# Mixture-of-experts stage: weights in row quarters of 1024 columns, gate before up, joins over two blocks

## The chip, the core and the metric

The kernel runs on one core of a Trainium2 chip. The metric is the device time of one execution in microseconds, as the median of three runs. The engines are TensorE (PE, matmul), VectorE (DVE), ScalarE (ACT), GpSimd (POOL) and SyncE (SP, which here only issues transfers).

## What is computed

One layer of a decoder, fp32 in and out, 1024 tokens of width 1024: normalisation and projection, two groups of attention heads, an output projection, and then a mixture of 32 experts, of which each token takes 4. The change lies in the experts:

```python
def moe_ffn(h, w_router, b_router, w_gate_up, b_gate_up, w_down, b_down):
...
    logits = (h @ w_router).astype(jnp.float32) + b_router.astype(jnp.float32)
    top_val, top_idx = lax.top_k(logits, TOP_K)
    gates = jax.nn.softmax(top_val, axis=-1)
...
    def expert_block(args):
        xe, e = args
        gu = xe @ w_gate_up[e] + b_gate_up[e]
        g = jnp.minimum(gu[:, :D_FF], SWIGLU_LIMIT)
        u = jnp.clip(gu[:, D_FF:], -SWIGLU_LIMIT, SWIGLU_LIMIT)
        act = (u + 1.0) * (g * jax.nn.sigmoid(SWIGLU_ALPHA * g))
        return act @ w_down[e] + b_down[e]
...
    y = yb[dest] * gate_sorted[:, None].astype(yb.dtype)
    return jax.ops.segment_sum(y, tok_sorted, num_segments=n)
```

The layer's output is `x + gate2 * y`, with `gate2` (the second gate) a row of 1024 that comes from the layer's condition `c`.

## The kernel before

**Stages.** The first 590 us or so are the projection and the attention, then come output projection and router by blocks of 128 tokens, which end in a list of tokens for every expert, and from about 743 us on the experts run one after the other. The order of the experts is by their load (`seq`), and each place in it has a fixed number of columns (tokens) `C`, from 200 down to 96 (`CAPS`). The order alternates, mostly a large one and a small one: 15 experts have at most 128 columns, that is one block, 17 have more, that is two blocks. The last one in time has 96.

**One expert.** `stage_g` gathers the rows of its tokens (POOL). `stage_t` turns them by PE transposes, four per bank of PSUM, and makes the operand `xx` out of them: ACT copies the high part, DVE subtracts to get the low part, POOL casts `xb`. `first_products` multiplies 512 rows x 512 columns of weights at a time (`kh` = 0, 1) into four banks: four high products per column block with `xx`, which carries high and low part side by side (2C columns, at least 256), and four low products with `xb` (C columns). A half of 512 columns of gate is followed by the same half of up, then the second halves follow. `joined` (L1177 to L1183) puts a block of sums together: ACT adds the bias into `tb` (L1179), DVE adds `tb` and the high sums (L1181, L1183). Gate goes through a sigmoid, two blocks at once (L1197, L1198). Down takes the raw fp32 weights (L1220; two records in the trace for each matmul), in two passes `kh` over two column halves, and after the first pass `between()` calls `stage_t` for the next expert. ACT empties the sums of down into `yT` (L1225). `back` turns `yT` back (L1237), DVE multiplies by the token's weight and by `gate2` (L1239), and POOL scatters into `out` with addition (L1153). `back` is put off to the first `done` of the next expert.

**Weights.** A chunk is 512 rows x 512 columns, 1 MB, issued by SP (`load_chunk`, L782). Chunks of gate and up have 5 tiles (`eraw`), those of down 4 (`draw`). A chunk of gate or up is split in two steps (`split_half`): ACT writes the high half (L796), DVE the low half in bf16 (L797), into 12 slots. `done(c)` runs after each chunk's products: it gives the chunk free and calls `pump`, which issues loads as long as tiles are free and writes up to one split (two after a chunk of down).

**Order.** In the expert stage PE, ACT, DVE and SP keep the order in which the program is written; POOL's order is the planner's.

Of the kernel before, what the change touches and what calls it, by code (L numbers as in the profile page):

```python
# [9 lines left out]
F32 = mybir.dt.float32  # L10
# [10 lines left out]
P = 128  # L21
# [37 lines left out]
ND = 4  # L59
# [7 lines left out]
TB = 2  # L67
# [6 lines left out]
NC_ = 512  # L74
# [3 lines left out]
def hybrid_layer(ctx: ExitStack, tc: tile.TileContext, x, c_t, w_ada, b_ada_t, b_ada, norm1_t, w_in,  # L78
# [11 lines left out]
    modd = dram.tile([3, D], F32, name="modd")  # L90
# [30 lines left out]
    def rsqrt_mean(*a):  # L121
# [18 lines left out]
    gate2 = consts.tile([P, D], F32, name="gate2")  # L140
# [43 lines left out]
    with ExitStack() as st:  # L184
        with ExitStack() as sp:
# [164 lines left out]
            def mod_row(n, acc):  # L350
# [11 lines left out]
                def rest():  # L362
                    if v == 3:
                        nc.vector.tensor_add(gate2[:, cs], pb, bb)
                        return
# [154 lines left out]
        with ExitStack() as so:  # L520
# [139 lines left out]
            m2 = rt.tile([P, 2, KT], F32, name="m2")  # L660
            wr = rt.tile([P, KT, E], F32, name="wr")
# [101 lines left out]
            at_ = {"dma": 0, "split": 0, "use": 0, "open": 0}  # L763
            raws, held = {}, {"eraw": 0, "draw": 0}
            pools = {"eraw": (wraw, NRAW)}
# [6 lines left out]
            def kind_of(d):  # L772
                return "eraw" if d % NCH < NGU else "draw"

            def load_chunk():
                d, kind = at_["dma"], kind_of(at_["dma"])
                i, w, n, kh = CHUNKS[d]
# [3 lines left out]
                raws[d] = pools[kind][0].tile([P, 4, NC_], F32, name=kind, bufs=pools[kind][1])  # L781
                nc.sync.dma_start(raws[d], w[ds(e, 1), kh * 512:(kh + 1) * 512, n * NC_:(n + 1) * NC_]  # L782
                                  .rearrange("o (k p) n -> p (o k) n", p=P))
                held[kind] += 1
                at_["dma"] += 1

            def split_half():

                t = at_["split"]
                c, q = t // 16 * NCH + t % 16 // 2, t % 2  # L790
                raw = raws[c][:, 2 * q:2 * q + 2]
                h_ = slot(False).rearrange("p (k n) -> p k n", k=2)
                if q == 0:
                    parts[c] = [], slot(True).bitcast(BF16).rearrange("p (k n) -> p k n", k=4)
# [625 lines left out]
```

## Time and profile before

| | us |
|---|---|
| median of 3 runs (2167.42 to 2168.32) | 2167.44 |
| the profiled execution | 2167.32 |
| its span, first to last instruction | 2165.5 |
| PE busy in the span | 2094.8 |
| DVE busy | 1499.6 |
| ACT busy | 1150.2 |
| POOL busy | 429.3 |

The profile is one execution on the chip. A line of a group gives source line, engine, operation, the tile written and the tiles read, the shape, the count, the busy time and the mean length of one instruction. A line of the timeline gives start and length of a run of like instructions, their count, and in brackets how long the engine had stood idle before and what ended that. The lengths of consecutive matmuls overlap in the timeline, so their pace is read from start to start. A view of stretches gives the busy time of every engine between two moments, the clock granted to PE, the busy share of the transfer engines and their rate.

### The profile page before, as it was taken

How to read it: one execution, taken by the hardware profiler on the slowest of the kernel's cores; microseconds unless marked ns; L12 is line 12 of the kernel's file. 1: busy time of each engine (PE TensorE's matmuls, PEld its weight loads, DVE VectorE, ACT ScalarE, POOL GpSimd, SP SyncE). 2: the span in 40 equal slices, each digit the busy share in tenths (PEclk: the TensorE clock that was granted, in tenths of full speed). 3: DMA queues.
4: the chain of work that ended last, by engine and by line, in shares of the span. 5: the costliest groups of instructions: out<-in, count | busy, mean ns of one | idle time of the engine just before them, and what ended most of it. 6: DMA issues, size and time to landing. Idle time of an engine off the chain costs nothing. (4 is left out here: it accounts for less than half of the span.)

```text
span 2165.5 us, 43655 instructions
## 1 busy us (share of the span) xinstructions
PE 2094.8 (97%) x16922; PEld 1957.5 (90%) x16922; DVE 1499.6 (69%) x2946; ACT 1150.2 (53%) x2263; POOL 429.3 (20%) x444
## 2 busy tenths in 40 slices
PE   7999999999999699999999999999999999999997
PEld 6877778998777699999999999999999999999997
DVE  6587756776666876677667677776767767667763
ACT  3522224777633455566456565656556656656652
POOL 2255532111045401111011111110111101101100
PEclk9999999999999799999999999999999999999999
DMA  7267886442224598799799999989989989999882
GB/s 294 73 163 215 221 230 172 114 109 76 89 105 153 192 356 299 247 334 350 255 292 326 300 314 319 332 312 343 315 297 312 361 297 320 323 315 335 297 320 60
DMA packets 272404, 548.98 MB, mean 254 GB/s; under 512 B 30675, under 2 KB 30691, under 8 KB 272067
## 3 DMA queue, kind: packets, MB, share of 16 engines
q1 hardware_dynamic: 250323, 490.09, 65.4%
q0 software_dynamic: 21872, 56.08, 11.1%
q8 instruction: 134, 2.20, 0.4%
q14 instruction: 75, 0.61, 0.1%
HBM read 501.31 MB, written 44.77 MB: 252 GB/s over the span
## 5 line engine op out<-in xcount | busy, mean ns | idle before, releaser
L797 DVE TENSOR_TENSOR ha<-eraw,hb 128x1024 bf16<-128x1024 f32 x512 | 601.3, 1224 | 233.5 <-ACT hb L796 233.0
L1167 PE MATMUL gu<-xx,hb 128*128 128x256 f32 (+13 forms) x4096 | 641.5, 304 | 0.6 <-DVE xx L1149 0.6
L1167 PEld LDWEIGHTS gu<-xx,hb 128*128 128x128 f32 x4096 | 561.1, 190 | 1.0 <-DVE xx L1149 0.8
L796 ACT ACTIVATE hb<-eraw 128x1024 fp32r<-128x1024 f32 x512 | 506.7, 1053 | 34.1 <-DMA eraw<-in_w_gate_up_dram 34.0
L1220 PE MATMUL gu<-aa,draw 128*128 128x128 f32 (+19 forms) x4096 | 521.2, 288 | 0.0
L1220 PEld LDWEIGHTS gu<-aa,draw 128*128 128x128 f32 x4096 | 511.2, 191 | 0.6
L1171 PE MATMUL gu<-xb,ha 128*128 128x128 bf16 (+19 forms) x4096 | 316.2, 224 | 0.0
L1179 ACT ACTIVATE tb<-gu,bcol 128x128 f32<-128x128 f32 (+19 forms) x512 | 164.6, 371 | 253.8 <-PE gu L1171 225.7
L1171 PEld LDWEIGHTS <-ha 128*128 128x128 bf16 x4096 | 246.6, 98 | 28.4 <-issue 3.3
L1153 POOL DMA_INDIRECT out_dram<-y,slot x47 | 81.6, 1736 | 528.3 <-DVE y L1239 251.4
L1126 POOL DMA_INDIRECT xg<-h2d,slot x47 | 54.5, 1160 | 629.0 <-PE gu L1146 381.8
L1225 ACT ACTIVATE yT<-gu,bcol 128x128 f32<-128x128 f32 (+19 forms) x256 | 82.4, 374 | 126.6 <-PE gu L1220 126.5
L572 DVE CUSTOM_DVE_ANT_0 p<-pss,bias 128x1024 f32<-128x1024 f32 (+7 forms) x128 | 94.4, 755 | 49.5 <-ACT p L581 22.2
L606 PE MATMUL po<-vsb,pT 128*128 128x64 f32 (+1 forms) x864 | 111.1, 275 | 2.6 <-ACT pT L600 1.5
L606 PEld LDWEIGHTS po<-vsb,pT 128*128 128x128 f32 x864 | 105.6, 194 | 4.8 <-ACT pT L600 1.8
L581 ACT ACTIVATE p<-p,mn 128x1024 f32<-128x1024 f32 (+7 forms) x128 | 98.6, 773 | 12.8 <-DVE mn L572 12.1
L1197 ACT ACTIVATE sg<-gt 128x256 f32<-128x256 f32 (+19 forms) x128 | 55.8, 436 | 89.2 <-DVE gt L1183 89.2
L461 PE MATMUL pp<-wh,hb 128*128 128x512 f32 x240 | 101.7, 424 | 0.0
L1198 DVE TENSOR_TENSOR gt<-gt,sg 128x256 f32<-128x256 f32 (+19 forms) x128 | 57.4, 448 | 63.4 <-ACT sg L1197 63.4
L112 POOL TENSOR_TENSOR rrs<-vrs,nhalf 128x8 f32<-128x8 f32 (+2 forms) x48 | 66.6, 1386 | 165.3 <-DVE vrs L110 160.2
L463 PE MATMUL pp<-wl,hb 128*128 128x512 f32 x240 | 94.9, 395 | 0.0
L462 PE MATMUL pp<-wh,hb 128*128 128x512 f32 x240 | 94.8, 395 | 0.0
(265 smaller groups left out, 2623.6 us busy)
## 6 DMA issues: line engine op xcount, KB each, us to landing
eraw<-in_w_gate_up_dram SPq DMA_DIRECT2D x256, 1024.0 KB
draw<-in_w_down_dram SPq DMA_DIRECT2D x128, 1024.0 KB
wraw<-in_w_ada_dram SPq DMA_DIRECT2D x32, 512.0 KB
wraw<-in_w_in_dram SPq DMA_DIRECT2D x23, 512.0 KB
hb<-in_w_ada_dram SPq DMA_DIRECT2D x16, 512.0 KB
qd<-tt POOLq DMA_DIRECT2D x32, 256.0 KB, 4.0
kd<-tt POOLq DMA_DIRECT2D x32, 256.0 KB, 4.2
ha<-qd SPq DMA_DIRECT2D x32, 256.0 KB
```

Source lines behind the costliest of these rows:

```text
L461: nc.tensor.matmul(pp, hh[b][:, k], wh[:, kk], start=(k == 0), stop=False)
L462: nc.tensor.matmul(pp, hl[b][:, k], wh[:, kk], start=False, stop=False)
L463: nc.tensor.matmul(pp, hh[b][:, k], wl[:, kk], start=False, stop=(k == KT - 1))
L572: nc.vector.tensor_tensor_reduce(p[:, :n], pss[:, :n], bias[:, (NB - 1 - ib) * P:(NB - 1 - ib) * P + n], -1.0, 3.0e38, OP.add, OP.min, mn)
L581: nc.scalar.activation(p, p, AF.Exp, bias=self.mn[c], scale=-1.0, accum_out=self.l[:, c:c + 1])
L606: nc.tensor.matmul(self.po[:, :w], self.pT[:, k], vsb[self.br][:, k, self.h * w:(self.h + 1) * w], start=(k == 0), stop=(k == self.ib))
L796: nc.scalar.activation(h_, raw, AF.Copy)
L797: nc.vector.tensor_tensor(l_, raw, h_.bitcast(F32), OP.subtract)
L1167: nc.tensor.matmul(pg[j][:, :max(256, 2 * C)], w[k][0][:, j * P:(j + 1) * P], xx[4 * kh + k], start=(kh + k == 0), stop=False)
L1171: nc.tensor.matmul(pg[j][:, C:2 * C], w[k][1][:, j * P:(j + 1) * P], xb[:, 4 * kh + k], start=False, stop=(kh == 1 and k == 3))
L1179: nc.scalar.activation(t, p[:, C:2 * C], AF.Identity, bias=bias, scale=1.0)
L1220: nc.tensor.matmul(p, w[:, k, j * P:(j + 1) * P], a[:, 4 * kh + k], start=(kh + k + j % 2 == 0), stop=(kh == 1 and k == 3 and j % 2 == 1))
```

## The change

Seen from the code, it does this:

- A chunk is now 256 rows x 1024 columns, still 1 MB. All kinds of chunks share one ring of 7 tiles. Gate and up have four chunks each per expert, down four. A split takes one half of a chunk's columns.
- Both halves of gate come first, then both halves of up. A product call (`products`) uses the splits of one column half from all four quarters of the rows.
- The low half of split t is written behind the high half of split t + 1. The number of splits that `pump` may write after each of the 12 `done()` events of an expert stands in the table `TG`.
- Tiles of PSUM are two banks. `joined` handles two blocks at once on DVE, the sigmoid four. `back` makes eight transposes and one evacuation, on ACT, with the token's weight as scale.
- `gate2` enters as scale and in the bias when ACT empties the sums of down (`g2c`, loaded from a fourth row of `modd`). The full row `gate2` is loaded only for the overflow stage at the end.
- Down goes by quarters of the rows over all 1024 columns. `between(0)` after the second quarter makes the first four transposes of each block of the next expert, `between(1)` after the fourth makes the other four and then `xx` and `xb`.
- `N3` is 0, so the code that stands under `if N3` and the terms with `N3` have no effect.

```diff
-ND = 4
+NRING = 7
+TG = (12, 12, 14, 16, 17, 18, 19, 20, 22, 24, 26, 27)
+N3 = 0
...
-    gate2 = consts.tile([P, D], F32, name="gate2")
-
-
-
-    CHUNKS0 = [(w_gate_up, 2 * u + half, kh) for half in range(2) for u in range(2) for kh in range(2)] + \
-              [(w_down, n, kh) for kh in range(2) for n in range(2)]
+
+
+
+    CHUNKS0 = [(w_gate_up, u, kq) for u in range(2) for kq in range(4)] + [(w_down, 0, kq) for kq in range(4)]
     NGU, NCH = 8, len(CHUNKS0)
+    NSP = 2 * NGU + (NCH - NGU if N3 else 0)
...
+                nc.sync.dma_start(g2c, modd[3].rearrange("(k p) -> p k", p=P))
...
+            def room():
+
+                d = at_["dma"]
+                p = pools.get(d % NRING >= NRAW)
+                return p if d < len(CHUNKS) and p and (d < NRING or d - NRING in freed) else None
...
+                raws[d] = pool.tile([P, 2, FF], F32, name=name, bufs=n)
+                nc.sync.dma_start(raws[d], w[ds(e, 1), kq * 256:(kq + 1) * 256, u * FF:(u + 1) * FF]
                                   .rearrange("o (k p) n -> p (o k) n", p=P))
...
+            def low(t):
+                c, half = chunk_of(t)
+                nc.vector.tensor_tensor(parts[t][1], raws[c][:, :, half * 512:(half + 1) * 512], parts[t][0].bitcast(F32), OP.subtract)
+                give(c, 1)
...
+                nc.scalar.activation(h_, raws[c][:, :, half * 512:(half + 1) * 512], AF.Copy)
+                if t:
+                    low(t - 1)
+                if t == E * NSP - 1:
+                    low(t)
...
+            def pump(upto):
+
                 while True:
-                    d, t = at_["dma"], at_["split"]
-                    kind = kind_of(d)
-                    if d < len(CHUNKS) and kind in pools and held[kind] < pools[kind][1]:
+                    if room():
                         load_chunk()
-                    elif t < limit and t // 16 * NCH + t % 16 // 2 < d and at_["open"] < NH:
+                    elif at_["split"] < upto and splittable():
                         split_half()
                     else:
                         return
...
+        def done(*ts):
+
+            used.update(ts)
+            for t in ts:
+                parts.pop(t)
+            i, q = divmod(event[0], len(TG))
+            event[0] += 1
+            pump(i * NSP + TG[q])
             for t in todo:
                 t[0] -= 1
             while todo and todo[0][0] <= 0:
...
+        def stage_t(st, g):
+
+            C = st["C"]
+            if g == 0:
+                st["x"], st["pt"] = operand(C, "xx", "xb"), []
+                bc = st["bc"]
+                nc.vector.tensor_mul(bc[:, 2 * KT:], bc[:, 2 * KT:], g2c)
+            xx, xb, _ = st["x"]
+            for (t0, n), xg in zip(st["blocks"], st["xg"]):
+                if g == 0:
+                    st["pt"].append(banks().rearrange("p g (k c) -> p (g k) c", k=4))
+                pt = st["pt"][t0 // P]
+                for k in range(4 * g, 4 * g + 4):
+                    nc.tensor.transpose(pt[:, k, :n], xg[:n, k * P:(k + 1) * P], ident[:n, :n])
+                if g:
+                    d_ = xx[:, :, t0:t0 + n]
                     nc.scalar.activation(d_, pt[:, :, :n], AF.Copy)
-                    nc.vector.tensor_sub(xx[:, 4 * g:4 * g + 4, C + t0:C + t0 + n], pt[:, :, :n], d_.bitcast(F32))
-                    nc.gpsimd.tensor_copy(xb[:, 4 * g:4 * g + 4, t0:t0 + n], d_.bitcast(F32))
+                    nc.vector.tensor_sub(xx[:, :, C + t0:C + t0 + n], pt[:, :, :n], d_.bitcast(F32))
+                    nc.gpsimd.tensor_copy(xb[:, :, t0:t0 + n], d_.bitcast(F32))
...
-        def joined(dst, p, C, bias, more=0.0):
-            t = ap_.tile([P, C], F32, name="tb", bufs=TB)
-            nc.scalar.activation(t, p[:, C:2 * C], AF.Identity, bias=bias, scale=1.0)
-            if more:
-                nc.vector.scalar_tensor_tensor(dst, t, more, p[:, :C], op0=OP.add, op1=OP.add)
-            else:
-                nc.vector.tensor_add(dst, p[:, :C], t)
-
...
+            def joined(dst, p, f, more):
+
+                t = ap_.tile([P, 2, C], F32, name="tb", bufs=2)
+                for j in range(2):
+                    nc.scalar.activation(t[:, j], p[:, j, C:2 * C], AF.Identity, bias=bc[:, f + j:f + j + 1], scale=1.0)
+                if more:
+                    nc.vector.scalar_tensor_tensor(dst, t, more, p[:, :, :C], op0=OP.add, op1=OP.add)
+                else:
+                    nc.vector.tensor_add(dst, p[:, :, :C], t)
...
+                ts = of(0, half)
+                pg = products(C, st["x"], ts)
+                gt = ap_.tile([P, 4, C], F32, name="gt", bufs=2)
                 for q in range(2):
+                    joined(gt[:, 2 * q:2 * q + 2], pg[q], 4 * half + 2 * q, 0.0)
+                sg = ap_.tile([P, 4, C], F32, name="su")
+                nc.scalar.activation(sg, gt, AF.Sigmoid, scale=1.702)
+                nc.vector.tensor_mul(gt, gt, sg)
+                gts.append(gt)
+                done(*ts[2:])
...
+            for kq in range(4):
+                raw = raws[d0 + kq]
+                for j in range(KT - N3):
+                    for k in range(2):
+                        nc.tensor.matmul(place(j), raw[:, k, j * P:(j + 1) * P], a[:, 2 * kq + k],
+                                         start=(kq + k + j % 2 == 0), stop=(kq == 3 and k == 1 and j % 2 == 1))
+                give(d0 + kq, 1 if N3 else 2)
...
+                    nc.gpsimd.tensor_copy(ab[:, f:f + 4], ah[:, f:f + 4, :C].bitcast(F32))
+                if kq == 3:
+                    for j in range(KT - N3):
+                        nc.scalar.activation(yT[:, j], place(j), AF.Identity,
+                                             bias=bc[:, 2 * KT + j:2 * KT + j + 1], scale=g2c[:, j:j + 1])
+                done()
+                if kq % 2:
+                    between(kq // 2)
...
+                    py = banks().rearrange("p g (k c) -> p (g k) c", k=4)
+                    for k in range(KT):
+                        nc.tensor.transpose(py[:n, k], yT[:, k, r0:r0 + n], ident)
+                    nc.scalar.activation(y[:n].rearrange("p (k c) -> p k c", k=KT), py[:n], AF.Copy, scale=sl[:n, 1:2])
...
-            expert(st, lambda: nxt and stage_t(nxt))
+            expert(i, st, lambda g: nxt and stage_t(nxt, g))
```

## Rows read from the trace of the kernel before

**Rows 1.** Page's busy table, and PE in the 40 slices of the span.
```profile
PE 2094.8 (97%) x16922; PEld 1957.5 (90%) x16922; DVE 1499.6 (69%) x2946; ACT 1150.2 (53%) x2263; POOL 429.3 (20%) x444
...
PE   7999999999999699999999999999999999999997
```

**Rows 2.** Stretches: length, busy PE, PEld, DVE, ACT, POOL (counts), PE clock, DMA share, GB/s.
```profile
743.00:2152.00 1409.00, 1409.00 (x13054) 1375.68 (x13054) 982.75 (x1623) 814.05 (x1499) 184.95 (x201) 1.00 0.90 307
```

**Rows 3.** Page's costliest groups: low halves of splits, high products, down.
```profile
L797 DVE TENSOR_TENSOR ha<-eraw,hb 128x1024 bf16<-128x1024 f32 x512 | 601.3, 1224 | 233.5 <-ACT hb L796 233.0
L1167 PE MATMUL gu<-xx,hb 128*128 128x256 f32 (+13 forms) x4096 | 641.5, 304 | 0.6 <-DVE xx L1149 0.6
...
L1220 PE MATMUL gu<-aa,draw 128*128 128x128 f32 (+19 forms) x4096 | 521.2, 288 | 0.0
```

**Rows 4.** Timeline, 180-column expert into 124-column: start, length, engine, line, operands, count [idle before].
```profile
1241.07 1.01 PE L1146 MATMUL gu<-ident,xg 124*128 124x124 f32 x8
1241.76 1.06 ACT L1148 ACTIVATE xx<-gu 128x496 fp32r<-128x496 f32 x2 [3.60 <-PE gu L1146]
...
1241.92 9.93 PE L1220 MATMUL gu<-aa,draw 128*128 128x180 f32 x64
1242.37 1.26 DVE L1149 TENSOR_TENSOR xx<-gu,xx 128x496 fp32r<-128x496 f32 x2 [1.24 <-ACT xx L1148]
...
1251.56 2.20 PE L1167 MATMUL gu<-xx,hb 128*128 128x256 f32 x16
1251.88 0.71 ACT L1225 ACTIVATE yT<-gu,bcol 128x180 f32<-128x180 f32 x2 [1.67 <-PE gu L1220]
...
1252.49 2.97 ACT L796 ACTIVATE hb<-eraw 128x1024 fp32r<-128x1024 f32 x3
```

**Rows 5.** Transfers: a first load, its use, and the rate of a stretch.
```profile
1.21 5.06 SPq L294 DMA_DIRECT2D hb<-in_w_ada_dram  x9
...
5.12 0.49 DVE L229 TENSOR_SCALAR acc<-hb,sc 128x512 f32<-128x512 f32 x1 [2.32 <-DMA hb<-in_w_ada_dram]
...
26.00:28.00 2.00, 2.00 (x11) 2.00 (x11) 2.00 (x2) 0.00 (x0) 2.00 (x1) 1.00 1.08 421
```

**Rows 6.** PE's clock at the head of the stage: stretches, then PE's timeline.
```profile
717.00:717.50 0.50, 0.00 (x0) 0.00 (x0) 0.50 (x2) 0.43 (x1) 0.30 (x1) 1.00 0.00 0
...
720.50:721.00 0.50, 0.50 (x4) 0.50 (x4) 0.43 (x3) 0.15 (x1) 0.49 (x1) 0.50 1.02 418
...
746.00:748.00 2.00, 2.00 (x12) 1.76 (x11) 2.00 (x2) 2.00 (x3) 1.16 (x1) 0.57 0.33 51
...
742.77 4.96 PE L1167 MATMUL gu<-xx,hb 128*128 128x344 f32 x16 [0.65 <-DVE xx L1149]
...
752.62 2.75 PE L1167 MATMUL gu<-xx,hb 128*128 128x344 f32 x16
```

**Rows 7.** PE's timeline of a 124-column expert: steps of up, down.
```profile
1165.29 2.15 PE L1167 MATMUL gu<-xx,hb 128*128 128x256 f32 x16
...
1168.15 1.21 PE L1167 MATMUL gu<-xx,hb 128*128 128x256 f32 x8
...
1182.74 7.36 PE L1220 MATMUL gu<-aa,draw 128*128 128x124 f32 x64
1189.93 1.67 PE L1146 MATMUL gu<-ident,xg 128*128 128x128 f32 x16
```

**Rows 8.** Timeline of gate's evacuation at 124 columns.
```profile
1260.45 0.60 ACT L1179 ACTIVATE tb<-gu,bcol 128x124 f32<-128x124 f32 x2
1260.58 0.42 DVE L1198 TENSOR_TENSOR gt<-gt,sg 128x248 f32<-128x248 f32 x1 [0.48 <-ACT sg L1197]
1260.91 0.47 DVE L1183 TENSOR_TENSOR gt<-gu,tb 128x124 f32<-128x124 f32 x2
...
1261.42 0.41 ACT L1197 ACTIVATE sg<-gt 128x248 f32<-128x248 f32 x1 [0.37 <-DVE gt L1183]
```

More of the change, by code (lines that the diff above doesn't have):

```diff
@@ L66 @@
 BORD = (7, 5, 3, 1, 0, 2, 4, 6)
-TB = 2
 CAP0 = 172
@@ L762, in hybrid_layer @@
             parts, reg = {}, {0: 0}
-            at_ = {"dma": 0, "split": 0, "use": 0, "open": 0}
-            raws, held = {}, {"eraw": 0, "draw": 0}
-            pools = {"eraw": (wraw, NRAW)}
+            at_ = {"dma": 0, "split": 0}
+            raws, freed, used = {}, set(), set()
+            pools = {0: (wraw, NRAW, "eraw")}
             def expert_of(i):
@@ L785, in load_chunk, with give, chunk_of, splittable @@
                 at_["dma"] += 1
+            def give(d, n):
+                left[d] = left.get(d, 2) - n
+                if left[d] == 0:
+                    raws.pop(d)
+                    left.pop(d)
+                    freed.add(d)
+            left = {}
+            def chunk_of(t):
+                i, r = divmod(t, NSP)
+                return (i * NCH + r // 2, r % 2) if r < 2 * NGU else (i * NCH + r - NGU, 1)
+            def splittable():
+                t = at_["split"]
+                return t < E * NSP and chunk_of(t)[0] < at_["dma"] and (t < NH or (t - NH in used and (t - NH) | 1 in used))
@@ L1185, in expert, with of @@
-        def expert(st, between):
+                    done(*ts[:2])
+            return pg
+        def expert(i, st, between):
             C, bc = st["C"], st["bc"]
             a = ap_.tile([P, KT, C], F32, name="aa")
+            s_a = operand(C, "ax", "ab") if N3 else None
+            t0, d0 = i * NSP, i * NCH + NGU
+            gts = []
+            def joined(dst, p, f, more):
[6 more added lines that the diff above has]
+                    nc.vector.tensor_add(dst, p[:, :, :C], t)
+            def of(u, half):
+                return [t0 + 8 * u + 2 * kq + half for kq in range(4)]
@@ L1200, in expert @@
-                done(c)
-                c, pg = first_products(st)
+                    joined(gt[:, 2 * q:2 * q + 2], pg[q], 4 * half + 2 * q, 0.0)
[4 more added lines that the diff above has]
+                done(*ts[2:])
+            for half in range(2):
+                ts = of(1, half)
+                pg = products(C, st["x"], ts)
+                ut_ = ap_.tile([P, 4, C], F32, name="su")
@@ new lines, in expert @@
+            if N3:
+                ts = [t0 + 2 * NGU + kq for kq in range(4)]
+                pg = products(C, s_a, ts)
+                for j in range(4):
+                    f, p = 4 + j, pg[j // 2][:, j % 2]
+                    t = ap_.tile([P, 2, C], F32, name="tb", bufs=2)[:, 0]
+                    nc.scalar.activation(t, p[:, C:2 * C], AF.Identity, bias=bc[:, 2 * KT + f:2 * KT + f + 1], scale=g2c[:, f:f + 1])
+                    nc.vector.scalar_tensor_tensor(yT[:, f], p[:, :C], g2c[:, f:f + 1], t, op0=OP.mult, op1=OP.add)
+                done(*ts[2:])
@@ L1298, in hybrid_layer @@
         lists(0)
-        pump(PB - at_["split"])
+        pump(PB)
         st = stage_g(0)
-        stage_t(st)
+        stage_t(st, 0)
+        stage_t(st, 1)
         lists(1)
-        pump(NH - at_["open"])
+        pump(TG[-1] - NSP)
         mans.close()
```

156 lines of the change are left out of this document (47 added, 109 removed).

## Prediction

> **What bounds the kernel now.** I looked first for the engine without slack. The page's busy table and its 40 slices give TensorE (PE) 97% of the span, and from the fifteenth slice on PE shows nine tenths or more in every slice [rows 1]. The view of stretches sharpens this: from 743 to 2152 us PE is busy 1409.00 us of 1409.00, at a granted clock of 1.00 [rows 2]. That stretch is the expert stage, 65% of the span, and nothing in it makes PE wait. Next comes what is in those 1409 us. By the groups of costliest instructions they are above all the high products of gate and up (L1167) and the down products (L1220), with 4096 records each [rows 3]; the low products (L1171) and the transposes come behind them. The change leaves every one of these matmuls, with its column count, in place: two records for each fp32 matmul of down, 256 matmuls of gate and up and 8 to 16 transposes in and out per expert. It follows that **there is nothing to win inside the stage**: the change can only alter the 756 us outside it or open holes in a full engine. So I read the rest of the trace for one purpose: what stands between the end of one expert and the first product of the next, and how much room it has.
>
> In the kernel before that room is large. The timeline of an expert with 180 columns followed by one with 124 shows the 8 transposes of the next expert's rows at 1241.07 in the middle of down, the two copies (ACT) and the two subtractions (DVE) that make its operand `xx` done by 1243.63, and the first product of the next expert only at 1251.56 [rows 4]. The operand is ready 8 us early.
>
> **The change part by part.** *Edits with no effect on PE.* DVE loses 2 of 4 joins per half and the `y` products with the gate; ACT gains one 1024-element evacuation per block. Neither engine is the bound (983 and 814 us of 1409 [rows 2]), and their work lies beside the products, so the saving is worth nothing; what covers it is the full PE. The rows of 4 KB instead of 2 KB for weights are worth nothing either: DMA moves 307 GB/s on average in the stage [rows 2] while PE waits for none of it, and rows of 2 KB reached 421 GB/s in the opening stage [rows 5]. The one extra write of `modd` on POOL, the small load `g2c` on SP and the late load of `gate2` lie in stages whose PE does not wait for those queues; with the longer first evacuation I put 2 us on start and end together (bounds 0 and 6; the start's own row is the 0.65 us of idle ahead of 742.77 [rows 6]).
>
> *The operand of the next expert.* This is the part that decides. `stage_t` is now called twice: four transposes per block after the second quarter of down, the other four **after the last one**, and only then the copy to `xx`, the subtraction and POOL's cast. PE runs in written order, and the next thing written on PE is the first gate product, which reads `xx`. Nothing else lies between: `back` comes only at the first `done` of the next expert. So at each of 31 expert boundaries PE stands still for a chain on ACT and DVE. Count it from the last down matmul, at the boundary of [rows 4] (T = 1251.56). ACT takes up the last pair of `yT` 0.32 us after T and needs 0.71: T+1.03. The `done()` that stands ahead of the second `stage_t` lets `pump` write one more weight split (limit 26 to 27), and ACT is served in order: + 0.99 (2.97 for 3): T+2.02. Copy to `xx` of 8 x 124: at most the two old copies, 1.06: T+3.08. Subtraction, likewise 1.26: T+4.34. PE meanwhile does four transposes, half of the 0.85 us that 8 took (1241.07 to 1241.92): 0.43. **Hole: 3.9 us.** For a following expert of two blocks another short copy and subtraction and another four transposes come in, which nearly cancel.
>
> After an expert of at most 128 columns the chain is longer, since a quarter of down is then short: 64 records in 7.2 us (1182.74 to 1189.93 [rows 7]), so 3.6 us for a quarter. The ring has 7 weight tiles, and the chunk that is split after quarter 3 can be requested only when quarter 2's predecessor has set its tile free, one quarter ahead. From issue to use a half-megabyte load took 3.9 us on an empty queue (1.21 to 5.12 [rows 5]); another half megabyte at 421 GB/s adds 1.2: 5.1 us, an estimate from these rows. So ACT gets the chunk 1.5 us after the quarter's end, splits two halves (2.0), does eight `yT` at about 0.3 (2.5) and stands at 6.0 where it would have been at 4.6. Hole: 3.9 + 1.4 = 5.3 us. With 14 boundaries after small experts and 17 after large: 14 x 5.3 + 17 x 3.9 = **140 us**. Bounds: 31 x 2.9 = 90 (the split out of the way) and 31 x 5.3 = 164.
>
> *The joins, and splits one step late.* The sigmoid now waits for all four blocks, and the low half of a split is written one split later. The second half of the first up product needs the low half of split 14, which `pump` writes after the sigmoid of the second gate half. At 124 columns: ACT's last pair 0.60, join 0.47, sigmoid over 496 elements about 0.6 and product about 0.7 (the halves take 0.41 and 0.42), then two low halves of 1.2 each [rows 3, 8]: 4.9 us after the gate's end. PE gets there after 16 + 16 matmuls (1165.29 to 1168.15 [rows 7]) and 8 more (half of the 2.15 for 16): 3.9. Hole 1.0 us. At 180 columns the sums are 5.5 and 5.3. With 15 experts at 1.0 and 17 between 0 and 0.6: **20 us**, bounds 0 and 40.
>
> *The clock.* After a hole PE may not run at its old rate. In the head of the stage the granted clock was 0.50 (1.2 GHz, the lower of its two levels) from 720.5 on; before that PE had no work at all from 717.0 to 717.5. It came back between 746 and 748, after PE had been at work from 742.77 without a pause [rows 6]. Under the lower clock a run of 16 products of 344 columns is 4.96 us long, at the full clock 2.75 [rows 6]: 2.2 us lost by one recovery. If each hole costs one, 31 x 2.2 = **68 us**; if none does, 0. No row shows dense work, one hole of 4 us and dense work again, so both ends stay; I take the full price, because the fall at 720.5 came without a hole of this length just ahead of it.
> The Trainium skill, "TensorE: Matmul & The Clock Gate", section "HAM oscillation — how this bites in real kernels", says the same of loops in which each pass ends with a wait: the clock falls in every pass and the slow restart is paid each time. By that rule the sum has the 68 us; without it, it hasn't. That a single hole in dense work does it, no run here shows yet.
>
> *Sum.* 140 + 20 + 68 + 2 = 230 us. The profiled execution took 2167.32 us (span 2165.5), 0.1 us from the median 2167.44, so I add to the median: **2397 us**.
>
> **The rivals.** *The clock holds* (everything else as above): 2167 + 162 = 2329 us. For it: in [rows 6] PE found the clock still at 1.00 while it stood, and lost it only 3 us later. Against it: a hole here is eight times the empty half microsecond of that row.
>
> *The loads starve the stage.* The ring falls from 9 tiles to 7, and `pump` frees none between the fifth step and the first quarter of down, so six chunks go out together at an expert's end. Six chunks and the next are 7.3 MB: 17.4 us at 421 GB/s [rows 5], 23.9 at the 307 GB/s that the stage now moves [rows 2]. The split that wants the seventh comes after five steps, some 16 us for 124 columns plus the hole. At 421 GB/s it waits hardly at all; at 307, 3 to 5 us, and PE behind it. 31 x 3 = 93 us or more on top: 2490 us. For it: the DMA share is already 0.90 [rows 2]. Against it: PE's holes themselves leave more time.
>
> *The boundary is covered after all* (not slower). Place: the copy to `xx` behind the last quarter. If the program that is built puts these copies before quarter 3's end, the 4.3 us chain would fit into the 3.6 to 4.9 us of a quarter, and with it the clock would hold; then 2167 to 2190 us, no difference from the point where the operand is done when PE ends down. This is also the case in which the change doesn't do what it says. Against it: ACT, DVE and PE are under the written order in this stage, and the trace of before obeys it everywhere I looked.
>
> *Part of the chain overlaps* (the split early, two thirds of a hole, clock held): 2167 + 90 = 2257 us.
>
> **How the numbers follow.** Chances: forecast 0.55 (own range 2350 to 2440), clock holds 0.25 (2285 to 2350), starved 0.08 (2450 to 2550), covered 0.06, part 0.06. The range 2285 to 2450 leaves out the last three, 0.20. A difference of 0.2%, 4.3 us, is about what a measurement can tell here from no change. Slower takes all cases but the covered one, and of that half: 0.95; the rest is split between same (0.03) and faster (0.02), the latter only if the 756 us outside the stage gain.
>
> **What would show it right or wrong.** Right: PE idle of 4 to 5 us ahead of the first gate product of each expert, released by DVE's subtraction into `xx`; ahead of it on ACT one split between the last `yT` and the copy to `xx`; a granted clock below 1.00 in the first 5 us of each expert; a hole of up to 1 us ahead of the low products of the first up half; the PE busy time outside the slow stretches unchanged. Wrong: a full PE at the boundaries (the covered case); a clock of 1.00 throughout (only 2329); idle ended by DMA rather than DVE (starved); a changed start-to-start time of the products at full clock, for which I have no price at all.

## The result, and the profile after

| | before | after |
|---|---|---|
| median, us | 2167.88 (2167.42 to 2168.36) | 2437.40 (2431.84 to 2447.09) |
| the profiled execution, us | 2167.32 | 2447.09 |
| its span, us | 2165.5 | 2445.3 |
| granted PE clock over the span | 0.989 | 0.946 |

The ratio of the medians is 1.1246, with a 95% interval of 1.1218 to 1.1274: the change costs 270 us. The forecast was 2397 us, slower, in the range 2285 to 2450. The direction, the place and the order of the terms came out; the sum was 40 us short.

Busy table and slices of the changed kernel, to be held against [rows 1]:

```profile
PE 2176.7 (89%) x16922; PEld 2023.6 (83%) x16922; DVE 1397.9 (57%) x2511; ACT 1211.6 (50%) x2199; POOL 419.7 (17%) x397
...
PE   7999999998987988889888888988888899898986
```

PE has as many instructions as before (16922), but its share falls from 97% to 89%, and the slices of the expert stage, nines before, are eights now. PE's busy time has also grown, by 82 us with the same instructions: it stands still, and it runs slower. The stretch of the stage, with the columns of [rows 2]:

```profile
743.00:2432.00 1689.00, 1492.36 (x13072) 1442.64 (x13072) 886.58 (x1189) 876.88 (x1438) 180.24 (x157) 0.94 0.79 257
```

The share of DMA falls from 0.90 to 0.79 and the clock from 1.00 to 0.94. Which work is late for PE, by the view of PE's waits from 780 to 2400 us (waiting line <- what it waited for: us in total, times, longest), and the page's groups of the gate and up products beside [rows 3]:

```profile
PE gu L1192 <- DVE xx L1173: 170.1, 31, 7.9
PE gu L1196 <- DVE ha L809: 18.8, 27, 0.9
```
```profile
L1192 PE MATMUL gu<-xx,hb 128*128 128x256 f32 (+13 forms) x4096 | 693.3, 321 | 172.3 <-DVE xx L1173 172.3
...
L1196 PE MATMUL gu<-xb,ha 128*128 128x128 bf16 (+19 forms) x4096 | 332.1, 229 | 19.8 <-DVE ha L809 19.7
```

All 31 boundaries between experts have a hole (a stretch in which PE stands idle) ahead of the first gate product, 5.5 us on average, and 27 experts have a small one ahead of the low products of up. **The 279.8 us of span** divide like this: the holes at the boundaries 170.1; the holes of the low products 18.8; the four groups of matmuls 73.9 more busy time (high products 641.5 to 693.3, low 316.2 to 332.1, down 521.2 to 524.5, transposes back 48.3 to 51.2); 10.3 because the first product comes at 753.03 instead of 742.77; and 1.1 at the tail, behind the last down product. That leaves 5.6. The transposes of the next expert's rows, which now come in two groups, are busy 47.3 us from the first product on, 40.6 before; these 6.7 are about that remainder (busy times of groups overlap at their ends, so such sums are not exact to a us). This profiled execution is the longest of the four, so the median has some 10 us less to divide.

One boundary in the timeline, to be held against [rows 4]: down of an expert of 140 columns, and the next one has 124 (start, length, engine, line, operands, count, [idle before]):

```profile
1235.90 2.00 ACT L820 ACTIVATE hb<-eraw 128x1024 fp32r<-128x1024 f32 x2 [3.06 <-DMA eraw<-in_w_gate_up_dram]
...
1236.96 0.59 PE L1169 MATMUL gu<-ident,xg 124*128 124x124 f32 x4
...
1237.81 2.96 ACT L1267 ACTIVATE yT<-gu,bcol,g2c 128x140 f32<-128x140 f32 x8
...
1240.63 1.09 ACT L820 ACTIVATE hb<-eraw 128x1024 fp32r<-128x1024 f32 x1
1241.58 1.03 ACT L1172 ACTIVATE xx<-gu 128x992 fp32r<-128x992 f32 x1
...
1242.64 1.19 DVE L1173 TENSOR_TENSOR xx<-gu,xx 128x992 fp32r<-128x992 f32 x1 [3.28 <-ACT xx L1172]
```
```profile
1229.33 7.79 PE L1256 MATMUL gu<-aa,eraw 128*128 128x140 f32 x64
...
1243.88 3.69 PE L1192 MATMUL gu<-xx,hb 128*128 128x256 f32 x16 [6.33 <-DVE xx L1173]
...
1252.94 2.15 PE L1192 MATMUL gu<-xx,hb 128*128 128x256 f32 x16
```

The chain is the one of the forecast: `yT`, one more split, copy to `xx`, subtraction, product. But ahead of it ACT had stood 3.06 us for a chunk that was late, and so all eight `yT` stand behind the end of down, not one pair. The second fence is PE's own timeline; its first line is the third and the last quarter of down together (a quarter has 32 records). The first 16 products behind the hole take 3.69 us, the same 16 take 2.15 nine microseconds later. The view of stretches shows why (columns as in [rows 2]; the last but two is the granted clock):

```profile
1238.00:1240.00 2.00, 0.00 (x0) 0.00 (x0) 1.35 (x2) 2.00 (x7) 1.05 (x1) 1.00 1.03 420
1240.00:1242.00 2.00, 0.00 (x0) 0.00 (x0) 0.00 (x0) 2.00 (x5) 0.00 (x0) 0.63 1.02 406
1242.00:1244.00 2.00, 0.12 (x1) 0.12 (x1) 1.36 (x2) 1.55 (x2) 1.01 (x1) 0.50 1.07 350
1244.00:1246.00 2.00, 2.00 (x10) 2.00 (x11) 0.96 (x1) 0.00 (x0) 0.00 (x0) 0.50 1.00 338
1246.00:1248.00 2.00, 2.00 (x19) 1.95 (x19) 0.00 (x0) 0.00 (x0) 0.00 (x0) 0.66 1.05 416
1248.00:1250.00 2.00, 2.00 (x26) 1.83 (x23) 0.00 (x0) 0.61 (x1) 0.00 (x0) 1.00 1.00 395
```

PE has been idle since 1237.55. The clock stays at 1.00 until 1240, falls to 0.50 (1.2 GHz) within the hole, and is back at 1.00 by 1248, after PE has worked again from 1243.88.

### The profile page after: what moved, and what is told of

Its sections match the earlier page's. It is cut to its first block, busy times and chain, and to the rows that moved or that the text cites. A ratio compares the mean times of both kernels' runs of the same rounds, so it can differ in the third digit from the quotient of the medians.

```text
span 2445.3 us, 42953 instructions
## 1 busy us (share of the span) xinstructions
PE 2176.7 (89%) x16922; PEld 2023.6 (83%) x16922; DVE 1397.9 (57%) x2511; ACT 1211.6 (50%) x2199; POOL 419.7 (17%) x397
## 4 chain that ended last, share of the span: by engine, by line
PE 46%; DMA 7%; ACT 7%; DVE 6%; issue 4%; SPq 0%; POOL 0%; ACTq 0%; POOLq 0%; DVEq 0%
PE gu L1192 21%; PE gu L1256 13%; PE gu L1196 9%; DMA draw<-in_w_gate_up_dram 4%; DMA eraw<-in_w_gate_up_dram 3%; DVE ha L809 3%; ACT hb L820 2%; ACT yT L1267 2%; PE gu L1287 2%; DVE xx L1173 2%; ACT xx L1172 1%; ACT tb L1213 1%; ACT su L1229 1%; PE gu L1169 0%; DVE gt L1217 0%
## 5 line engine op out<-in xcount | busy, mean ns | idle before, releaser
L1192 PE MATMUL gu<-xx,hb 128*128 128x256 f32 (+13 forms) x4096 | 693.3, 321 | 172.3 <-DVE xx L1173 172.3
L809 DVE TENSOR_TENSOR ha<-eraw,hb 128x1024 bf16<-128x1024 f32 x366 | 431.3, 1219 | 81.0 <-ACT hb L820 81.0
L820 ACT ACTIVATE hb<-eraw 128x1024 fp32r<-128x1024 f32 x366 | 371.3, 1055 | 183.9 <-DMA eraw<-in_w_gate_up_dram 183.8
L1256 PE MATMUL gu<-aa,eraw 128*128 128x128 f32 (+19 forms) x2944 | 375.9, 288 | 0.0
L1256 PEld LDWEIGHTS gu<-aa,eraw 128*128 128x128 f32 x2944 | 367.7, 191 | 0.4
L1196 PE MATMUL gu<-xb,ha 128*128 128x128 bf16 (+19 forms) x4096 | 332.1, 229 | 19.8 <-DVE ha L809 19.7
L1217 DVE TENSOR_TENSOR gt<-gu,tb 128x256 f32<-128x256 f32 (+19 forms) x128 | 57.3, 447 | 341.0 <-ACT tb L1213 340.9
L820 ACT ACTIVATE hb<-draw 128x1024 fp32r<-128x1024 f32 x146 | 148.7, 1053 | 144.6 <-DMA draw<-in_w_gate_up_dram 144.3
L809 DVE TENSOR_TENSOR ha<-draw,hb 128x1024 bf16<-128x1024 f32 x146 | 173.3, 1220 | 71.9 <-ACT hb L820 71.9
L1256 PE MATMUL gu<-aa,draw 128*128 128x124 f32 (+16 forms) x1152 | 148.6, 288 | 0.0
L1256 PEld LDWEIGHTS gu<-aa,draw 128*128 128x128 f32 x1152 | 144.7, 191 | 0.4 <-ACT hb L820 0.2
L1267 ACT ACTIVATE yT<-gu,bcol,g2c 128x128 f32<-128x128 f32 (+19 forms) x256 | 96.3, 468 | 43.7 <-PE gu L1256 43.6
```

Of the source, the lines that this page charges most:

```text
L809: nc.vector.tensor_tensor(parts[t][1], raws[c][:, :, half * 512:(half + 1) * 512], parts[t][0].bitcast(F32), OP.subtract)
L820: nc.scalar.activation(h_, raws[c][:, :, half * 512:(half + 1) * 512], AF.Copy)
L1192: nc.tensor.matmul(pg[j // 2][:, j % 2, :max(256, 2 * C)], w[k][0][:, j * P:(j + 1) * P], xk[4 * kh + k], start=(kh + k == 0), stop=False)
L1196: nc.tensor.matmul(pg[j // 2][:, j % 2, C:2 * C], w[k][1][:, j * P:(j + 1) * P], xb[:, 4 * kh + k], start=False, stop=(kh == 1 and k == 3))
L1256: nc.tensor.matmul(place(j), raw[:, k, j * P:(j + 1) * P], a[:, 2 * kq + k], start=(kq + k + j % 2 == 0), stop=(kq == 3 and k == 1 and j % ...
L1267: nc.scalar.activation(yT[:, j], place(j), AF.Identity, bias=bc[:, 2 * KT + j:2 * KT + j + 1], scale=g2c[:, j:j + 1])
```

## The experiments

All ratios are to the kernel before in the same series of runs (its medians: 2166.45, 2167.99 and 2166.18). The changed kernel was measured in a series of its own, so a difference to its 2437.40 us is one between series, and their kernels before lie within 1.8 us.

**The place of the operand, in the old kernel.** The theory: the late operand alone makes the holes and their clock, so the kernel before with `between()` behind all of down must lose most of the 270 us. The rival: it needs the new chunks, joins or ring.

```diff
-                if kh == 0:
-                    between()
+
+            between()
```

> The kernel before with one edit: the operand of the next expert is made behind the last chunk of down instead of in the middle of it. Theory 1: a hole of 3.9 to 4.9 us at each of 31 boundaries (two or three splits stand ahead of the copies on ACT) and a recovery of the clock of 2.2 us each: 2355 to 2390 us. Rival (the cost belongs to the new order of chunks and the smaller ring, not to the place of the operand): below 2200 us.

Measured 2357.65 us, 1.0881 (1.0863 to 1.0899). Waits of PE and the high products:

```profile
PE gu L1167 <- DVE xx L1149: 121.3, 31, 4.3
```
```profile
L1167 PE MATMUL gu<-xx,hb 128*128 128x256 f32 (+13 forms) x4096 | 689.3, 319 | 122.0 <-DVE xx L1149 122.0
```

There are 31 holes of 3.9 us. The high products take 47.8 us more, the low ones 15.7 more (331.9 for 316.2) and the transposes back 2.3 more (50.6 for 48.3). The theory holds: one moved call costs 191 us, against the 270 of the whole change.

**The place mended, in the changed kernel.** All eight transposes and the operand after the second quarter of down, as before the change.

```diff
-                if kq % 2:
-                    between(kq // 2)
+                if kq == 1:
+                    between(0)
+                    between(1)
```

> The changed kernel with one edit: both parts of the next expert's operand are made after the second quarter of down instead of after the second and the fourth. Theory 1 (the place of the operand is what costs, the ring of 7 weight tiles suffices): the 31 holes ahead of the first gate product (170 us) and the slow clock behind them (about 80 us) go, the holes ahead of the low products of up (19 us) and the later start stay: 2195 to 2205 us. Theory 2 (the loads are late as well, and the hole at the boundary only hides it): PE then waits elsewhere, above all at the start of down, behind ACT's splits that wait for DMA: 2250 to 2310 us.

Measured 2292.91 us, 1.0586 (1.0569 to 1.0604). The holes at the boundary are gone and the high products are back at 642.3 us, so they were the cause of both. But 126 us remain, and the theory that only small things were left (2195 to 2205) falls. In the profiled execution 81 us of what remains are waits of PE in the stage, and 26 are longer down products (547.5 us for 521.2), which stand behind most of these waits. PE's longest waits, then ACT's for DMA:

```profile
PE gu L1256 <- ACT hb L820: 51.1, 20, 7.2
PE gu L1196 <- DVE ha L809: 19.1, 28, 0.9
```
```profile
ACT hb L820 <- DMA eraw<-in_w_gate_up_dram: 293.6, 66, 13.9
ACT hb L820 <- DMA draw<-in_w_gate_up_dram: 165.9, 36, 10.7
```

and one place in the timeline, PE's and ACT's:

```profile
1114.52 1.06 ACT L820 ACTIVATE hb<-draw 128x1024 fp32r<-128x1024 f32 x1 [10.15 <-DMA draw<-in_w_gate_up_dram]
1115.48 1.12 ACT L1213 ACTIVATE tb<-gu,bcol 128x128 f32<-128x128 f32 x4
```
```profile
1117.58 10.08 PE L1256 MATMUL gu<-aa,eraw 128*128 128x128 f32 x64 [4.29 <-ACT hb L820]
```

ACT stands 10.15 us at a split whose chunk has not landed; behind it in ACT's order are the evacuations of the last up products; down waits for what is made of them; PE has a hole of 4.29 us. ACT waits 459.5 us for weights in all (293.6 + 165.9), against 328.1 in the changed kernel and 34.0 before. So the late loads of the rival were there all along: the holes at the boundaries had given the loads time, and had hidden most of their cost.

**One tile more in the ring.** `NRING` 7 to 8, nothing else. If the boundary's chain is alone at fault, no difference; if late chunks lengthen it, the holes shrink to the chain.

```diff
-NRING = 7
+NRING = 8
```

> The changed kernel with a ring of 8 weight tiles instead of 7, nothing else. If the part of the hole beyond my count (5.5 us against 4.5) comes from chunks that arrive after the quarter of down in which they were asked for, ACT's waits for DMA (328 us in the changed kernel) fall below 100 us, the hole to 3.7 to 4.0 us each, and the time to 2380 to 2395 us. If late chunks play no part: 2437 us, holes unchanged.

Measured 2406.97 us, 1.1105 (1.1087 to 1.1124). PE's waits at the boundary, and ACT's for weights:

```profile
PE gu L1192 <- DVE xx L1173: 131.2, 31, 4.7
```
```profile
ACT hb L820 <- DMA eraw<-in_w_gate_up_dram: 28.4, 12, 7.1
...
ACT hb L820 <- DMA draw<-in_w_gate_up_dram: 12.3, 7, 3.5
```

ACT's wait falls from 328 to 41 us and the holes from 170.1 to 131.2, now of 4.2 us each. So 39 of the 170 us came from late chunks and 131 from the chain itself. The holes and the time came out above what I had expected: the medians differ by 30 us only. Nothing came back from the clock (high products 692.0 us, of 693.3): a hole of 4.2 us costs as much clock as one of 5.5.

**Mended place and eight tiles.**

> The changed kernel with the operand made after the second quarter of down and a ring of 8 weight tiles. With the operand early alone it took 2293 us and PE waited 51 us ahead of down behind ACT's splits, which waited for DMA. Theory (one more tile takes the loads off the path): those waits go, and their slow clock; left are 19 us ahead of the low products of up and the later start of the stage: 2195 to 2210 us. Rival (the order of the loads, with nothing freed between the fifth step and down, starves the stage whatever the ring): 2250 us or more.

Measured 2226.15 us, 1.0267 (1.0250 to 1.0284), 67 us less than the mended place with seven tiles, but 16 us above the expectation. ACT still waits 123.6 us for weights (122.3 + 1.3), and some of it reaches PE: four waits of down, 16.7 us in all. The holes of the low products are there too, 29 times, 19.8 us, none over 0.9. And the high products take 641.6 us, as before the change: **holes of 0.9 us cost no clock**, while in the changed kernel holes of 4 to 8 us cost the same group 52 us.

**The low half at once.** The low half of a split behind its own high half, in the changed kernel.

```diff
-                if t:
-                    low(t - 1)
+                low(t)
                 at_["split"] += 1
-                if t == E * NSP - 1:
-                    low(t)
```

> The changed kernel with the low half of each split written right behind its high half, not one split later. Theory: the holes ahead of the low products of the first up half (19 us, 27 times) go to nearly 0, and nothing else changes; chunks also come free one split sooner, which may take some of the late loads off the boundary: 2405 to 2420 us. Rival (the holes there come from DVE's joins over two blocks): holes stay at 19 us, 2437 us.

Measured 2418.93 us, 1.1159 (1.1141 to 1.1178). No wait of a low product is left; the holes at the boundaries stay (173.0 us, 31 times). The medians differ by 18.5 us, and the waits that are gone had 18.8 (besides, the low products are 4.2 us shorter, 327.9, and the holes at the boundaries 2.9 longer in all).

**The split behind the copy.** At the last quarter, `between(1)` ahead of `done()`, so that ACT makes `xx` before the split.

```diff
+                if kq == 3:
+                    between(1)
                 done()
-                if kq % 2:
-                    between(kq // 2)
+                if kq == 1:
+                    between(0)
```

> The changed kernel with one exchange: after the last quarter of down the operand's second part is written ahead of done(), so that the weight split that done() lets through stands behind the copy to the operand on ACT, not ahead of it. By my chain this split is 1.0 us of each hole, and more where it waits for its chunk: holes of 4.0 to 4.5 us instead of 5.5, 2390 to 2410 us. Rival (the copy waits for DVE or for sums, not for ACT's turn): 2437 us.

Measured 2407.27 us, 1.1106 (1.1083 to 1.1129), with 131.7 us in 31 holes: 1.2 us less each. That is about one split (0.99 in [rows 4]). It doesn't separate the split's own length from its chunk's lateness: a late chunk can still hold up the splits of the quarter before, and with them `yT`, but the split that the last quarter releases now stands behind the copy.

**The clock kept up.** 16 idle products of 512 columns ahead of the first gate product of each expert but the first, from a split that is already there, into a bank that the real products then clear. They do nothing for the result.

```diff
+            for _ in range(fill):
+                f_ = parts[ts[0]][0][:, 0]
+                nc.tensor.matmul(pg[0][:, 0], f_[:, :P], f_, start=True, stop=True)
...
-                pg = products(C, st["x"], ts)
+                pg = products(C, st["x"], ts, 16 if i and half == 0 else 0)
```

> The changed kernel with 16 idle products of 512 columns (0.22 us each) ahead of the first gate product of each expert, into a bank of sums that the real products clear; they need nothing but weights that are ready. They fill about 3.5 us of each hole with work that nobody uses. If the growth of PE's busy time (82 us) is the slow clock after a hole, most of it goes: 2365 to 2390 us, with granted clock near 1.00 behind the holes. If that growth has another cause, the time stays at 2437 us or rises.

Measured 2398.61 us, 1.1078 (1.1058 to 1.1098), 39 us below the changed kernel although PE has 496 products more; a little above the expectation. The granted clock over the span is 0.981 instead of 0.946. PE's waits, then the high products:

```profile
PE gu L1195 <- DVE xx L1173: 37.7, 28, 3.8
PE gu L1199 <- DVE ha L809: 19.8, 29, 0.9
PE gu L1188 <- ACT yT L1270: 15.3, 9, 3.3
```
```profile
L1195 PE MATMUL gu<-xx,hb 128*128 128x256 f32 (+13 forms) x4096 | 648.7, 306 | 40.0 <-DVE xx L1173 40.0
```

The high products come back from 693.3 to 648.7 us, of 641.5 before. The operand's chain is what it was; only PE's idleness is less. So the longer busy time is the clock, and the idle PE is what lowers it. Some holes are left (the filling itself waits for a bank nine times), and with them 7 us.

**All three mended.** Place, low half and eight tiles; then nine tiles, for which one temporary of the joins (`tb`) has one buffer instead of two.

```diff
-NRING = 7
+NRING = 9
...
-                t = ap_.tile([P, 2, C], F32, name="tb", bufs=2)
+                t = ap_.tile([P, 2, C], F32, name="tb", bufs=1)
```

> The changed kernel with three edits: operand after the second quarter of down, ring of 8 tiles, low half right behind its high half. Theory: no hole is left in the expert stage; what remains against the kernel before is the later first product of the stage (some 10 us) and nothing else, because joins over two blocks, the gate in ACT and 4 KB rows change no time of PE: 2170 to 2185 us. Rival (these parts cost or gain by themselves): above 2195 us, or below 2163 us.

> The changed kernel with the operand after the second quarter of down, the low half right behind the high half, and 9 weight tiles, which is as many as the kernel before has (to make room, one buffer less for the bias sums). With 8 tiles it took 2214 us, PE waited 22.6 us ahead of down and the clock dropped behind that. Theory (what is left is late loads): the waits fall to below 8 us, 2175 to 2195 us. Rival (what is left is the order in which chunks are asked for, which more tiles don't change): 2205 to 2215 us.

Eight tiles: 2213.86 us, 1.0217 (1.0193 to 1.0240). Nine: 2200.08 us, 1.0153 (1.0136 to 1.0170). Both above their expectations, by some 29 and 5 us. PE's waits, with eight tiles and with nine:

```profile
PE gu L1253 <- DVE aa L1239: 22.6, 6, 7.0
```
```profile
PE gu L1253 <- DVE aa L1239: 12.4, 3, 5.4
```

The high products take 641.3 and 641.0 us, the low ones 319.1 and 318.9. ACT waits for weights 118.5 us with eight tiles (117.5 + 1.0) and 67.0 with nine (56.2 + 10.8). The time with eight tiles lies in the rival's range: of the 46 us that are left, 22.6 are these waits and some 10 are longer down products (530.9 us for 521.2). With nine it lies between the theory's range and the rival's, and the waits are above the 8 us expected, so the order of the loads is not excluded as a cause. The stretches with eight tiles ahead of one such wait show how the loads come (last two columns: DMA share, GB/s), and then SP's loads and ACT's split there:

```profile
1118.00:1123.00 5.00, 5.00 (x47) 5.00 (x47) 2.99 (x4) 2.22 (x6) 1.91 (x2) 1.00 0.72 203
...
1138.00:1143.00 5.00, 5.00 (x55) 4.77 (x54) 3.38 (x4) 2.57 (x3) 0.00 (x0) 1.00 1.03 418
1143.00:1148.00 5.00, 5.00 (x56) 4.87 (x54) 0.00 (x0) 0.00 (x0) 0.00 (x0) 1.00 1.02 407
1148.00:1153.00 5.00, 1.67 (x18) 1.42 (x16) 1.18 (x2) 2.27 (x6) 0.10 (x1) 1.00 0.99 390
```
```profile
1124.32 3.51 SPq L784 DMA_DIRECT2D eraw<-in_w_down_dram  x4
...
1128.07 0.37 SPq L784 DMA_DIRECT2D eraw<-in_w_gate_up_dram  x1
```
```profile
1150.73 1.06 ACT L820 ACTIVATE hb<-eraw 128x1024 fp32r<-128x1024 f32 x1 [9.85 <-DMA eraw<-in_w_gate_up_dram]
```

The transfers bunch: 203 GB/s while little is given free, then all that fits, around 400, and for 5 us ACT and DVE have nothing to split. The chunk that ACT stands for was asked for at 1128.07, right behind the four chunks of down, and is there 22.7 us later. A ring with more tiles takes part of this away: in the kernels with the mended place the wait of ACT goes from 459.5 to between 118.5 and 123.6 and to 67.0 us, and the time from 2292.91 to 2226.15, and with the low half mended too to 2213.86 and 2200.08. The order over the tiles is as the theory has it, the last step smaller than expected. The step from eight to nine changes `tb` too; ACT then waits 52.8 us for DVE at that buffer, and what this takes from the gain was not measured by itself. No variant beats the kernel before.

**The part that should be worth nothing.** In the kernel before, the `y` product goes from DVE to ACT, with the token's weight as scale; the factor `gate2` is left out.

```diff
-                        nc.vector.scalar_tensor_tensor(y[:n, cs], py[:n], sl[:n, 1:2], gate2[:n, cs],
-                                                       op0=OP.mult, op1=OP.mult)
+                        nc.scalar.activation(y[:n, cs], py[:n], AF.Copy, scale=sl[:n, 1:2])
```

> The kernel before with only the evacuation of the turned-back rows moved from DVE to ACT, in the same two halves per block, with the token's weight as scale; the product with the second gate is left out. Theory (engines beside a full PE cost nothing): 2164 to 2172 us. Rival (ACT's turns are late and PE waits for sums): above 2175 us.

Measured 2166.83 us, 1.0003 (0.9993 to 1.0012). Work moved between two engines that are not the bound is worth nothing, as forecast.

## Why the prediction was right, and where its sizes were off

**The bound and the idle parts.** "Nothing to win inside the stage" held. Moving `y` to ACT changed 0.03%; wherever the holes at the boundaries were mended, the high products returned to 641.0 to 642.3 us, so new chunk shapes, wider banks and wider joins neither shorten nor lengthen them. Two small costs were not in the forecast: the transposes of the rows are busy 47.8 to 50.7 us in all eight variants of the changed kernel, 43.6 before, and down 524.5 us in the changed kernel, 521.2 before. What makes them was not tested. Rows of 4 KB moved up to 420 GB/s (from 1238 to 1240 us, above), rows of 2 KB 421 [rows 5]; no run changed the rows alone.

**The boundary: 140 us forecast, 170.1 measured.** The step is right: PE's waits name the subtraction into `xx`, the chain is the one that was counted, and the place alone costs 191 us in the old kernel and, with its clock, all but 126 us in the new one. But 170.1 is above the upper bound of 164 that the forecast gave this term, and two of its sizes were off.
- The chain after a large expert was forecast at 3.9 us. With eight tiles, where hardly a chunk is late, the holes are 4.2 (131.2 / 31). The difference is in the `yT`. The forecast has one pair behind the end of down, done 1.03 us later, from [rows 4]. In the kernel with eight tiles, at the same boundary as the one shown, four stand there (PE's timeline, then ACT's):

```profile
1224.03 0.59 PE L1169 MATMUL gu<-ident,xg 124*128 124x124 f32 x4
1228.88 3.35 PE L1192 MATMUL gu<-xx,hb 128*128 128x256 f32 x14 [4.27 <-DVE xx L1173]
```
```profile
1224.23 1.54 ACT L1267 ACTIVATE yT<-gu,bcol,g2c 128x140 f32<-128x140 f32 x4 [0.36 <-PE gu L1256]
```

  They are done at 1225.77, 1.74 us after PE has turned to the transposes; split, copy and subtraction then follow as counted.
- Late chunks were forecast at 20 us (14 x 1.4), and measured at 39 (170.1 - 131.2). The estimate of 5.1 us from issue to use came from an almost empty queue and a single transfer of half a megabyte. At the boundary shown, the chunk is the first of these four loads (SP's timeline), and it took 7.05 us, up to 1235.90:

```profile
1228.85 4.86 SPq L784 DMA_DIRECT2D eraw<-in_w_gate_up_dram  x4
```

  The third quarter ends near 1233.2, half-way through the 7.79 us of the last two quarters. So the two splits that are written behind it begin 2.7 us after its end and not 1.5, and all eight `yT` come after them. And this is an expert of 140 columns: lateness isn't confined to the small ones, as the forecast had it.

**The joins and late low halves: 20 us forecast, 18.8 measured**, in 27 waits of at most 0.9 us. The low half written at once takes them all away and 18.5 us with them.

**The clock: 68 us forecast, 65 to 71 measured.** The full price was the right end. High products, low products and transposes back are busy 70.6 us longer (51.8 + 15.9 + 2.9). In the kernel with the operand early and eight tiles, which has no hole at a boundary, 64.6 of these are gone (641.6, 321.4 and 49.0 us). The 3.3 us of down are not the clock's: they stay with the idle products too (524.6 us). Per boundary that is 2.1 to 2.3 us, where the forecast took 2.2 from [rows 6]; the idle products show that it is the clock. This also settles what no row of before could: one hole of 4 us in dense work is enough, at each of the 31 boundaries. The Trainium skill, "TensorE: Matmul & The Clock Gate", section "HAM oscillation — how this bites in real kernels", says that a long enough wait for data in every pass of a loop lowers the clock in every pass and that the slow restart is paid each time; the trace agrees, with 0.50 from 1242 to 1246 at the hole shown. Here too it depends on the hole's length: 29 of at most 0.9 us left the high products at 641.6 us (the low ones, behind them, took 321.4 us, and 319.1 without these holes).

**Start and end: 2 us forecast, 11.4 measured in the profiled execution.** This edit was costed nearly at nothing, and too low. Ahead of the stage's first product stand two gathers of rows (POOL), their transposes, and the chain to `xx`. PE's waits from 700 to 800 us in the changed kernel, then PE's timeline:

```profile
PE gu L1169 <- DMA xg<-h2d,slots: 10.3, 2, 6.8
```
```profile
748.51 2.25 PE L1169 MATMUL gu<-ident,xg 44*128 44x44 f32 x12 [3.47 <-DMA xg<-h2d,slots]
753.03 2.37 PE L1192 MATMUL gu<-xx,hb 128*128 128x344 f32 x7 [2.27 <-DVE xx L1173]
```

Of the 10.3 us by which the first product is later, 4.6 lie ahead of the first gather (735.39 for 730.84). In the eight variants of the changed kernel it is issued between 729.09 and 731.74, so this belongs to the one execution rather than to the change. The other 5.7 do recur: from the first gather to the first product it is 17.6 us here, 16.0 to 20.3 in those eight, and 11.9 before. Start and end together are thus above the forecast's upper bound of 6 in this execution, and a little above it without the 4.6 (6.8). Of the 5.7, 1.6 us is the hole ahead of the first product, 2.27 for 0.65 [rows 6]: the copies now come behind all the transposes, where before they ran between them. For the rest there was a suspect, the order on POOL, which the planner makes: here the second gather comes behind four scatters, before it came ahead of them. It isn't enough. In the kernel with the low half at once and in those with all three mended both gathers are ahead of the scatters, and it is 16.0 to 17.1 us all the same. Why the rows land later there is open.

**The rivals.** *The clock holds* (2329) fell with the fall to 0.50. *The boundary is covered* fell: PE is held up at every one of the 31. *Part overlaps* (2257) likewise. *The loads starve the stage* is the instructive one. As a time (2490) it didn't come, and PE's waits in the changed kernel name DVE, not a weight. But its mechanism was in the kernel: it gave 39 us of the boundary's holes, and with the place mended it costs more by itself, 67 us between seven tiles and eight (2292.91 - 2226.15). The argument that stood against it, that PE's holes leave the loads time, was exactly right, and for this reason the two costs don't add up: 191 for the place and 126 for what is left when it is mended make more than the 270 of both.

**What in it was luck, and three slips.** Two terms passed their own upper bounds, the boundary and the start, and the clock stands at its own; that the total stayed in the range is owed to the joins, which took 18.8 of the 40 us allowed, and to a range that ends a little above the sum of the bounds. Three slips in the working move nothing much. The last slice of PE is a 7 [rows 1], since PE's work ends with the stage, before the span does. The chain of the joins at 124 columns adds up to 4.8 us and not 4.9. And by the rule that is given for it the chance of slower is 0.97, where the forecast says 0.95.

**Still open.** With nine tiles 34 us are left: 12.4 in three waits, about 10 in the down products (531.4 us for 521.2), 2.7 in the low products, 3.9 in the transposes of the rows (44.5 us for 40.6 from the first product on) and 6.1 at the start. The three waits (1152, 1338 and 1694 us) come where with eight tiles the longest ones were (1154, 1341 and 1700), which speaks for the loads' order; with nine tiles it wasn't followed up which load is the first late one.

## What to carry to other kernels

Before moving a step that makes the next stage's operand, count the chain from the last instruction of the full engine to its next one: 4 us of chain behind a full PE cost 6.2 us per boundary here (191 us over 31), a third of it from the clock. When a wait is mended, read again what the other queues were doing in its shadow; a ring of loads that the full engine hardly waits for may owe it to that engine's standing still.

## What the runs showed of the hardware

- In the hole shown PE kept a granted clock of 1.00 for over 2 us and then fell to 0.50, and a fall came at each of the 31 holes of 4 to 8 us; waits of at most 0.9 us, 29 times, cost no clock (high products 641.6 us). One fall costs 2.1 to 2.3 us in these products, hardly more behind holes of 5.5 us than behind 4.2 (high products 693.3 and 692.0 us).
- Idle products in the hole are worth it: 496 of them gave back 39 us.
- With eight tiles the weights moved at 203 GB/s in one stretch and at 390 to 418 in later ones: a mean of 302 GB/s in that stage (743 to 2150 us) told nothing of ACT's 118 us of waits.
